# A transformer layer on one core: the residual computed later, look-ups with written-out indices, and half chunks spread over the gate stage

## The chip, the cores and the metric

The kernel runs on one core of one Trainium2 chip. The metric is the device time of one execution in microseconds (us); the median of three executions of the kernel before is 2918.57 us (2915.17 to 2919.74). The engines of the core are PE (matrix products), DVE (vector), ACT (scalar functions and copies), POOL (general, here above all an issuer of DMAs) and SP (issues DMAs). Each runs its own instructions in order.

## The reference

One layer over 1024 tokens (and 16 meta tokens in front) of width 1024, all in float32:

```
h = layer_norm(concat(meta, x))                       # "embedding" norm with gain g and bias b
q, k, v, xr, gr = split(h @ w_in)                     # 3 x 512 and 2 x 512 columns
attn  = stick_breaking_attention(q, k, v)             # 8 heads of 64
lru   = rg_lru(conv4(xr)) * gelu(gr)                  # gated linear recurrence
h = layer_norm(ALPHA * h + concat(rms(attn), rms(lru)) @ w_out)
# PEER: 16384 experts, 8 heads, product keys of 2 x 128
s1, s2 = q1 @ keys1, q2 @ keys2                       # 128 scores each, per head
top 16 of each; top 16 of the sums -> 16 experts (i1 * 128 + i2) and softmax weights g
ffn = sum over heads, experts of g * gelu(down[e] . h) * up[e]
out = layer_norm(ALPHA * h + ffn)
```

## The kernel before

The tokens are 8 blocks of 128. Exact products are made of three reduced ones: every operand x is split into a high part (ACT, L123: wh, dh, v, uh) and a low part (DVE, L124: wl, dl, v, ul), and `mm3` (L126 to L129) issues low·high, high·high, high·low. What PE multiplies in a stage must thus have passed ACT and then DVE. Instructions have an order per engine that is set when the program is built, by a list scheduler that works with estimated durations; on the chip each engine takes its own list strictly in order and waits where an operand is missing.

*Start.* The norm runs in three batches of three blocks (`LNB`): DVE statistics, ACT normalises (L281), PE transposes, ACT applies gain and bias (L292), and hT is stored as high and low part (L295, L297, L298). Beside it `convs` makes the first two projections. Then the residual ALPHA * h is made in token order: `xts[j]` times eg plus eb (L303 to L308; 16 DVE operations on 128x1024), stored to DRAM as `xh_d` by SP, and read again by `lru_load` (L561) when the output projection runs, after the attention.

*Values and recurrence.* `values_w` splits value weights, `values` makes vt in 9 blocks per half, between the pieces of the recurrence (`lru_in`, `lru_gates`). Attention, output projection and second norm follow.

*Query stage* (`queries`). For each of 8 heads and both halves PE makes qt (three pieces, evacuated by ACT, L784) and the scores; DVE takes the top 16 (`topk1`), then of the sums (`topk_pos`), and `topk_look` turns positions into indices: `oh` compares a position with 0 to 15 (L744, against the constant `iotb`), is multiplied by the index repeated 16 times (L745), and is summed by halving (L746 to L749). Between, PE makes chunks of the dense product ahead of time (`run_ahead`, L861; number per step in `RAQ`), and DVE makes dot products with gathered rows (`hyb`).

*Gate stage.* For the 5 dense blocks of tokens the weights are spread over the 16384 experts: 80 groups of 8 tokens, each with two kinds of one-hot tables (DVE: bt, ae; ACT: at, eight copies at L1027), eight matmuls g (L1030), one evacuation (ACT, L1031), one `hyb` step, and one turn of the top-k of the last two blocks (`topk_turn`). After each block `RAG[j]` chunks (6, 7, 6, 6, 6, together 31) are made with `run_ahead`: a chunk is the down product of 128 experts with 640 tokens, two halves of 24 matmuls (dps), a gelu (ACT) and a store of 320 KB to `ge_d`. Four groups fill a gate buffer st, which SP stores to Gd (L1035).

*Dense stage.* 128 chunks: those made ahead (56, `RA`) are loaded from `ge_d`, the others are made here; each is multiplied by its gates (gl, L1142), split, and multiplied by the up rows (ups). Beside it DVE works through the gathered rows of the last blocks (`sparse_units`), given out in proportion to PE's work (`tick`).

## Time and profile before

| | |
|---|---|
| median of 3 executions | 2918.57 us |
| profiled execution, its span | 2921.73 us, 2919.9 us |
| busy: PE, DVE, ACT, POOL | 95%, 85%, 39%, 42% |
| mean granted clock of PE | 0.979 |
| start and norm, then values and recurrence | to about 54 us, to about 240 us |
| attention, output projection | to about 555 us, to about 625 us |
| query stage | 624 to 1047 us |
| gate stage, to the first up matmul | 1047.5 to 1504 us |
| dense stage and last norm | 1504 to 2919.9 us |

The profile names instructions by line of the kernel and by tile (out<-in). Busy shares are of the whole span; a view cut to a window tells what limits a stage. "Idle before" is the time for which an engine had nothing running before an instruction, with the releaser that ended it. A granted clock of 1.0 is 2.4 GHz, 0.5 is 1.2 GHz.

### The profile page before, as it was taken

How to read it: one execution, taken by the hardware profiler on the slowest of the kernel's cores; microseconds unless marked ns; L12 is line 12 of the kernel's file. 1: busy time of each engine (PE TensorE's matmuls, PEld its weight loads, DVE VectorE, ACT ScalarE, POOL GpSimd, SP SyncE). 2: the span in 40 equal slices, each digit the busy share in tenths (PEclk: the TensorE clock that was granted, in tenths of full speed). 3: DMA queues.
4: the chain of work that ended last, by engine and by line, in shares of the span. 5: the costliest groups of instructions: out<-in, count | busy, mean ns of one | idle time of the engine just before them, and what ended most of it. 6: DMA issues, size and time to landing. Idle time of an engine off the chain costs nothing.

```text
span 2919.9 us, 44345 instructions
## 1 busy us (share of the span) xinstructions
PE 2771.6 (95%) x16311; PEld 2490.4 (85%) x16311; DVE 2468.0 (85%) x4768; ACT 1146.0 (39%) x2245; POOL 1224.4 (42%) x1028
## 2 busy tenths in 40 slices
PE   5999999999899987999999999999999999999997
PEld 5998777789899986989988888888888888888886
DVE  8345666769999999689869999999999999999996
ACT  5444554552122268578832222222222232222232
POOL 0002320232333444134325565665555566666653
PEclk9999999999999999899999999999999999999999
DMA  5113134414677778698889999999999999999981
GB/s 176 46 59 88 42 88 151 145 57 148 224 240 230 246 235 276 202 290 252 262 292 351 349 347 353 345 351 361 343 350 355 350 337 358 360 342 369 334 312 73
DMA packets 353946, 736.32 MB, mean 252 GB/s; under 512 B 26032, under 2 KB 164272, under 8 KB 353728
## 3 DMA queue, kind: packets, MB, share of 16 engines
q0 software_dynamic: 113152, 411.16, 39.7%
q1 hardware_dynamic: 235968, 320.23, 32.6%
q8 instruction: 128, 2.10, 0.3%
q10 hardware_dynamic: 4608, 2.10, 0.3%
q14 instruction: 90, 0.74, 0.1%
HBM read 645.24 MB, written 79.69 MB: 248 GB/s over the span
## 4 chain that ended last, share of the span: by engine, by line
PE 50%; DVE 15%; issue 6%; POOL 3%; ACT 3%; DMA 2%; SPq 0%; POOLq 0%; DVEq 0%; ACTq 0%
PE dps L127 6%; PE dps L129 6%; PE dps L128 6%; PE ups L127 6%; PE ups L128 6%; PE ups L129 6%; PE g L1030 5%; DVE row L113 4%; POOL row L898 3%; DVE dl L124 2%; PE keep L129 2%; PE keep L128 2%; PE keep L127 2%; ACT gst L1031 1%; DMA row<-down,idx 1%
## 5 line engine op out<-in xcount | busy, mean ns | idle before, releaser
L127 PE MATMUL dps<-hTd,dl 128*128 128x320 f32 x2048 | 645.2, 315 | 33.8 <-DVE dl L124 26.1
L129 PE MATMUL dps<-hTd,dh 128*128 128x320 f32 x2048 | 641.2, 313 | 0.0
L128 PE MATMUL dps<-hTd,dh 128*128 128x320 f32 x2048 | 641.0, 313 | 0.0
L898 POOL DMA_INDIRECT row<-down,idx x256 | 357.7, 1397 | 226.1 <-DVE act L113 182.0
L898 POOL DMA_INDIRECT row<-up,idx x256 | 343.7, 1342 | 229.2 <-DVE h1s L1086 192.0
L127 PEld LDWEIGHTS dps<-hTd,dl 128*128 128x128 f32 x2048 | 388.9, 190 | 38.4 <-DVE dl L124 20.2
L127 PE MATMUL ups<-uh,wl 128*128 128x512 f32 x1024 | 406.3, 397 | 0.4 <-DVE wl L124 0.4
L128 PE MATMUL ups<-uh,wh 128*128 128x512 f32 x1024 | 406.3, 397 | 0.0
L129 PE MATMUL ups<-ul,wh 128*128 128x512 f32 x1024 | 405.5, 396 | 0.0
L128 PEld LDWEIGHTS dps<-hTd,dh 128*128 128x128 f32 x2048 | 388.9, 190 | 3.0
L129 PEld LDWEIGHTS dps<-hTd,dh 128*128 128x128 f32 x2048 | 388.3, 190 | 0.1
L1086 DVE SCALAR_TENSOR_TENSOR h1s<-row,gws,h1s 128x1024 f32<-128x1024 f32 x256 | 328.3, 1282 | 16.1 <-DMA row<-up,idx 14.0
L113 DVE CUSTOM_DVE_ANT_0 row<-row,h1s 128x1024 f32<-128x1024 f32 x256 | 307.5, 1222 | 33.9 <-DMA row<-down,idx 33.1
L123 ACT ACTIVATE wh<-gl 128x640 fp32r<-128x640 f32 x128 | 101.3, 792 | 575.9 <-DVE gl L1142 315.0
L898 POOL DMA_INDIRECT row<-up,idh x128 | 189.7, 1482 | 305.5 <-DVE acc L1076 95.8
L898 POOL DMA_INDIRECT row<-down,idh x128 | 162.2, 1268 | 245.1 <-DVE ach L113 106.3
L124 DVE TENSOR_TENSOR dl<-raw,dh 128x1024 fp32r<-128x1024 f32 x144 | 179.7, 1248 | 80.5 <-ACT dh L123 80.0
L129 PEld LDWEIGHTS ups<-ul,wh 128*128 128x128 f32 x1024 | 192.8, 188 | 47.3
L127 PEld LDWEIGHTS ups<-uh,wl 128*128 128x128 f32 x1024 | 192.8, 188 | 45.2 <-DVE wl L124 0.8
L128 PEld LDWEIGHTS ups<-uh,wh 128*128 128x128 f32 x1024 | 192.8, 188 | 43.9
L123 ACT ACTIVATE uh<-raw 128x1024 fp32r<-128x1024 f32 x128 | 133.5, 1057 | 191.1 <-PE keep L128 171.2
L1176 DVE TENSOR_TENSOR acc<-acc,ups 128x512 f32<-128x512 f32 x252 | 171.9, 682 | 16.8 <-PE ups L129 16.6
(577 smaller groups left out, 5948.1 us busy)
## 6 DMA issues: line engine op xcount, KB each, us to landing
raw<-downT SPq DMA_DIRECT2D x128, 512.0 KB
raw<-up SPq DMA_DIRECT2D x128, 512.0 KB
Gd<-gst SPq DMA_DIRECT2D x20, 2048.0 KB
gl<-Gd SPq DMA_DIRECT2D x128, 320.0 KB
ge_d<-ge SPq DMA_DIRECT2D x56, 320.0 KB
gex<-ge_d SPq DMA_DIRECT2D x56, 320.0 KB
wraw<-w_in SPq DMA_DIRECT2D x20, 512.0 KB
raw<-wq SPq DMA_DIRECT2D x16, 512.0 KB
```

The costliest lines, as they stand in the source:

```text
L113: return lambda *a, **k: pin(getattr(V, name)(*a, **k))
L123: A.activation(hi, src, AF.Copy)
L124: V.tensor_tensor(lo, src, hi.bitcast(F32), op=ALU.subtract)
L127: PE.matmul(o, ll, rh, start=start, stop=False, **kw)
L128: PE.matmul(o, lh, rh, start=False, stop=False, **kw)
L129: PE.matmul(o, lh, rl, start=False, stop=stop, **kw)
L898: G.indirect_dma_start(out=row, out_offset=None, in_=src, in_offset=bass.IndirectOffsetOnAxis(ap=ix, axis=0))
L1030: PE.matmul(gpt[:, q], bt[:, q], at[:, q], start=True, stop=True)
L1031: A.activation(st[:, :, t8 - t0:t8 - t0 + 8].rearrange("p a t b -> p t a b"), gpt.rearrange("p t (a b) -> p t a b", b=2), AF.Copy)
L1086: pin(V.scalar_tensor_tensor(h1s[:, j], row, gws[:, j, s:s + 1], h1s[:, j], op0=ALU.mult, op1=ALU.add))
L1176: V.tensor_tensor(h1[j][:, hsl], h1[j][:, hsl], ps, op=ALU.add)
```

## The change

Four things. First, SP now stores the normalised block itself (without gain and bias) to `xh_d`, and a generator `residuals` reads it back in half width on POOL's queue, applies gain and bias on DVE, and stores the result to a new `xr_d`; a step of it is taken after each block of `values`. Its tile `rt` has one buffer. Second, in the query stage ACT writes the index sixteenfold (`ibx`), so that the multiplication has a second operand that is read densely; `iotb` holds one table instead of six, and `oh` has one buffer instead of two. Third, 34 instead of 31 chunks are made ahead in the gate stage, by halves: 68 half chunks are given out evenly over the 80 groups (`ahead_turn`). Fourth, the dense stage thus has 3 chunks less to make (RA is 59). Lines below the first hunk move: L744 and L745 become L766 and L767, L1030 becomes L1072.

```diff
@@
 RAQ = {i: 1 + (i > 7) for i in range(1, 16)}
-RAG = (6, 7, 6, 6, 6)
+RAG = 34
 RAM = {7: 2}
-RA = sum(RAM.values()) + sum(RAQ.values()) + sum(RAG)
+RA = sum(RAM.values()) + sum(RAQ.values()) + RAG
 RAS = sorted([1 + 4 * i for i in range(min(RA, 32))] + [2 + 4 * i for i in range(RA - 32)])
@@
     xh_d = dram.tile([S, D], F32, name="xh_d")
+    xr_d = dram.tile([S, D], F32, name="xr_d")
     al_d = dram.tile([KC, P, S], F32, name="al_d")
@@
                     A.activation(xts[j][:n], xts[j][:n], AF.Identity, bias=nm9[:n, j:j + 1], scale=rs9[:n, j:j + 1])
+                    if j > 0:
+                        SY.dma_start(xh_d[(j - 1) * P:j * P, :], xts[j])
                 c0 = 0 if j0 == 0 else NM + (j0 - 1) * P
@@
                     next(gen)
-            eg = load_vec(ga, 0, "eg")
-            eb = load_vec(ga, 1, "eb")
-            A.activation(eg, eg, AF.Copy, scale=ALPHA)
-            A.activation(eb, eb, AF.Copy, scale=ALPHA)
-            for j in range(1, NT + 1):
-                V.tensor_tensor(xts[j], xts[j], eg, op=ALU.mult)
-                V.tensor_tensor(xts[j], xts[j], eb, op=ALU.add)
-                SY.dma_start(xh_d[(j - 1) * P:j * P, :], xts[j])
-
         with ExitStack() as c2:
@@
                 mps = c3.enter_context(tc.tile_pool(name="mps", bufs=1, space=PSUM, reuse_waits="tile"))
+                rx = c3.enter_context(tc.tile_pool(name="rx", bufs=1, reuse_waits="tile"))
                 sp8 = lr.tile([P, 4], F32, name="sp8")
@@

+                def residuals():
+                    for hf in range(2):
+                        cs = slice(hf * 512, hf * 512 + 512)
+                        gb = []
+                        for i in range(2):
+                            t = rx.tile([P, 512], F32, name=f"rv{i}")
+                            G.dma_start(t, vecs[i, cs].partition_broadcast(P))
+                            A.activation(t, t, AF.Copy, scale=ALPHA)
+                            gb.append(t)
+                        for j in range(NT):
+                            t = rx.tile([P, 512], F32, name="rt")
+                            G.dma_start(t, xh_d[j * P:(j + 1) * P, cs])
+                            V.tensor_tensor(t, t, gb[0], op=ALU.mult)
+                            V.tensor_tensor(t, t, gb[1], op=ALU.add)
+                            G.dma_start(xr_d[j * P:(j + 1) * P, cs], t)
+                            yield
+
+                res = residuals()
+
                 def lru_in(i):
@@
                         A.activation(vt[:m, b, half * 256:half * 256 + 256], ps[:m, :256], AF.Copy)
+                        next(res, None)

@@
                     V.tensor_tensor_scan(ts_[i], rs_[i], ys[i], 0.0, op0=ALU.mult, op1=ALU.add)
+                for _ in res:
+                    pass
                 ms = mps.tile([P, NT], F32, name="ms")
@@
                 hr = wr.tile([P, D], F32, name="raw")
-                SY.dma_start(hr, xh_d[j * P:(j + 1) * P, :])
+                SY.dma_start(hr, xr_d[j * P:(j + 1) * P, :])
                 return mh, ml, hr
@@
         tkw = c1.enter_context(tc.tile_pool(name=f"tkw{n}", bufs=wb, side=side, reuse_waits="tile"))
-        iotb = tk.tile([P, n, TOPK, TOPK], BF16, name=f"iotb{n}")
-        G.iota(iotb, pattern=[[0, n], [1, TOPK], [0, TOPK]], base=0, channel_multiplier=0, allow_small_or_imprecise_dtypes=True)
+        iotb = tk.tile([P, TOPK, TOPK], BF16, name=f"iotb{n}")
+        G.iota(iotb, pattern=[[1, TOPK], [0, TOPK]], base=0, channel_multiplier=0, allow_small_or_imprecise_dtypes=True)
         return tk, tkw, iotb
@@
         W.tensor_copy(ib, ii)
+        ibx = []
+        for half in range(2 if n > ST else 0):
+            t = tkw.tile([P, n, TOPK, TOPK], BF16, name="ibx")
+            A.activation(t, ib[:, half].unsqueeze(3).broadcast_to([P, n, TOPK, TOPK]), AF.Copy)
+            ibx.append(t)
         for half in range(2):
             oh = tkw.tile([P, n, TOPK, TOPK], BF16, name="oh", bufs=ohb)
-            W.tensor_tensor(oh, ab[:, half].unsqueeze(2).broadcast_to([P, n, TOPK, TOPK]), iotb[:, :n], op=ALU.is_equal)
-            G.tensor_tensor(oh, oh, ib[:, half].unsqueeze(3).broadcast_to([P, n, TOPK, TOPK]), op=ALU.mult)
+            W.tensor_tensor(oh, ab[:, half].unsqueeze(2).broadcast_to([P, n, TOPK, TOPK]), iotb.unsqueeze(1).broadcast_to([P, n, TOPK, TOPK]), op=ALU.is_equal)
+            G.tensor_tensor(oh, oh, ibx[half] if ibx else ib[:, half].unsqueeze(3).broadcast_to([P, n, TOPK, TOPK]), op=ALU.mult)
             G.tensor_tensor(oh[:, :, 0:8], oh[:, :, 0:8], oh[:, :, 8:16], op=ALU.add)
@@
             hs = slice(h * TOPK, (h + 1) * TOPK)
-            topk_look(V, tkw, iotb, DT, ab, ii, [sel[:, half, :, hs] for half in range(2)], V, 2)
+            topk_look(V, tkw, iotb, DT, ab, ii, [sel[:, half, :, hs] for half in range(2)], V, 1)
             yield
@@
     def down_gelu(c, dps, ge, tick=None):
+        for _ in down_halves(c, dps, ge, tick):
+            pass
+
+    def down_halves(c, dps, ge, tick=None):
         hi, lo = ddn.pop(c)
@@
                 tick(KC * 3 * HN)
+            yield

...

+    def aheads(n):
+        for _ in range(n):
+            c = next(ra)
+            ddn[RAS[c]] = take()
+            ge = geps[0].tile([P, NF], F32, name="ge")
+            for i, _ in enumerate(down_halves(RAS[c], dps1, ge)):
+                if i == 1:
+                    SY.dma_start(ge_d[c], ge)
+                yield
+
     def run_ahead():
-        c = next(ra)
-        ddn[RAS[c]] = take()
-        ge = geps[0].tile([P, NF], F32, name="ge")
-        down_gelu(RAS[c], dps1, ge)
-        SY.dma_start(ge_d[c], ge)
+        for _ in aheads(1):
+            pass

@@
                 turn[1] += 1
+
+        ahead = aheads(RAG)
+        gone = [0]
+
+        def ahead_turn(groups):
+            while gone[0] * groups < turn[0] * 2 * RAG:
+                next(ahead, None)
+                gone[0] += 1

@@
                     topk_turn(DF * P // 8)
+                    ahead_turn(DF * P // 8)
                 blk = (j * P + t0) // GB
                 SY.dma_start(Gd[:, :, blk].rearrange("g p f -> p g f"), st.rearrange("p (g a) t b -> p g (a t b)", a=GI // 2))
-            for c in range(RAG[j]):
-                run_ahead()
+        next(ahead, None)
         hdepth[0] = 0
```

Below, a row is engine order, line, operation, out<-in, shape; "x2" stands for two alike. First DVE at the end of the norm, before: xt are the residual's blocks, y the convolution, v the low part of the value weights, which PE needs next.

```order
L298 TENSOR_TENSOR hT_88<-tm,hT_87 128x384
L306 TENSOR_TENSOR xt<-xt,eg 128x1024 x2
L307 TENSOR_TENSOR xt<-xt,eb 128x1024 x2
L306 TENSOR_TENSOR xt<-xt,eg 128x1024 x2
L307 TENSOR_TENSOR xt<-xt,eb 128x1024 x2
L352 TENSOR_SCALAR y_631<-xr,ch 128x1040
L333 MEMSET t_630 128x4
L352 TENSOR_SCALAR y_632<-xr,ch 128x1040
L354 SCALAR_TENSOR_TENSOR y_631<-xr,ch,y_631 128x1040
L329 TENSOR_SCALAR t_628<-t_627 128x4
L124 TENSOR_TENSOR v_678<-wraw,v_677 128x8x128
```

And after (rt is the residual in half width):

```order
L354 TENSOR_TENSOR rt<-rt,rv_724 128x512
L301 TENSOR_TENSOR hT_89<-tm,hT_88 128x384 x3
L298 CAST hT_88<-tm 128x384
L355 TENSOR_TENSOR rt<-rt,rv_727 128x512
L301 TENSOR_TENSOR hT_89<-tm,hT_88 128x384
L328 MEMSET t_612 128x4
L125 TENSOR_TENSOR v_660<-wraw,v_659 128x8x128
L366 TENSOR_SCALAR y_613<-xr,ch 128x1040
L324 TENSOR_SCALAR t_610<-t_609 128x4
L368 SCALAR_TENSOR_TENSOR y_613<-xr,ch,y_613 128x1040
L325 RECIPROCAL t_610<-t_610 128x4
L125 TENSOR_TENSOR v_660<-wraw,v_659 128x8x128
```

The residual operations no longer stand between the last hT and v; two of the sixteen steps are seen among the hT rows, each with a load in front on POOL's queue.

Second, PE in the gate stage, where the first block's groups go on; before:

```order
L127 MATMUL dps<-hTd_5239,dl 128x320
L128 MATMUL dps<-hTd_5239,dh 128x320
L129 MATMUL dps<-hTd_5240,dh 128x320
L106 MATMUL tr<-ident,sf 128x128 x2
L106 MATMUL tr<-ident,gwd 128x128
L1030 MATMUL g<-at__11171,bt 128x128 x8
L685 MATMUL sc<-sk,qx 128x128 x2
L1030 MATMUL g<-at__11199,bt 128x128 x8
L1030 MATMUL g<-at__11239,bt 128x128 x8
L685 MATMUL sc<-sk,qx 128x128 x2
L1030 MATMUL g<-at__11643,bt 128x128 x8
```

and after:

```order
L129 MATMUL dps<-hTd_5314,dh 128x320
L130 MATMUL dps<-hTd_5315,dh 128x320
L128 MATMUL dps<-hTd_5314,dl 128x320
L129 MATMUL dps<-hTd_5314,dh 128x320
L1072 MATMUL g<-at__11810,bt 128x128
L130 MATMUL dps<-hTd_5315,dh 128x320
L1072 MATMUL g<-at__11810,bt 128x128 x2
L128 MATMUL dps<-hTd_5314,dl 128x320
L1072 MATMUL g<-at__11810,bt 128x128 x3
L129 MATMUL dps<-hTd_5314,dh 128x320
L1072 MATMUL g<-at__11810,bt 128x128 x2
L130 MATMUL dps<-hTd_5315,dh 128x320
```

Before, the down matmuls end here, and groups follow each other until the block is done; after, 24 down matmuls stand between (and partly within) one group's eight g and the next's.

Third, ACT in the query stage of head 7, which also holds the look-up of head 6; before:

```order
L861 ACTIVATE ge<-dps 128x320 x2
L123 ACTIVATE dh<-raw 128x1024
L861 ACTIVATE ge<-dps 128x320 x2
L123 ACTIVATE dh<-raw 128x1024
L784 ACTIVATE qt<-z 128x320 x2
L784 ACTIVATE qt<-z 128x384
L123 ACTIVATE dh<-raw 128x1024
L687 ACTIVATE sb<-sc 128x512
L687 ACTIVATE sb<-sc 128x256
```

and after:

```order
L887 ACTIVATE ge<-dps 128x320 x2
L124 ACTIVATE dh<-raw 128x1024
L887 ACTIVATE ge<-dps 128x320 x2
L124 ACTIVATE dh<-raw 128x1024
L806 ACTIVATE qt<-z 128x320 x2
L762 ACTIVATE ibx<-ib 128x1536 x2
L806 ACTIVATE qt<-z 128x384
L704 ACTIVATE sb<-sc 128x512
L124 ACTIVATE dh<-raw 128x1024
L704 ACTIVATE sb<-sc 128x256
```

Both writes of ibx stand between the second and the third piece of qt.

## Rows read from the trace of the kernel before

**Rows 1.** The page, part 1: busy time and share of the span by engine, instructions.
```profile
PE 2771.6 (95%) x16311; PEld 2490.4 (85%) x16311; DVE 2468.0 (85%) x4768; ACT 1146.0 (39%) x2245; POOL 1224.4 (42%) x1028
```

**Rows 2.** Windows: length; busy by engine (instructions); TensorE's clock, DMA share, GB/s.
```profile
60.00:80.00 20.00, 10.74 (x48) 8.56 (x48) 17.70 (x25) 6.61 (x10) 0.55 (x4) 0.61 0.44 148
80.00:240.00 160.00, 158.30 (x1084) 153.75 (x1083) 59.20 (x77) 70.59 (x100) 4.62 (x11) 1.00 0.19 54
640.00:1044.00 404.00, 373.30 (x2473) 371.28 (x2472) 388.71 (x1565) 95.61 (x169) 136.04 (x125) 0.97 0.64 207
1047.50:1504.00 456.50, 410.62 (x2798) 396.22 (x2796) 376.19 (x974) 341.69 (x840) 152.79 (x109) 0.96 0.82 262
1184.00:1232.00 48.00, 48.00 (x323) 48.00 (x323) 22.05 (x57) 19.29 (x45) 5.50 (x6) 0.96 0.60 203
1316.00:1374.00 58.00, 55.10 (x403) 52.52 (x402) 52.76 (x136) 52.28 (x131) 24.79 (x15) 0.99 0.79 244
1504.00:2840.00 1336.00, 1331.63 (x6897) 1164.01 (x6896) 1255.71 (x1546) 350.15 (x461) 796.79 (x583) 1.00 0.95 348
```

**Rows 3.** Waits of PE, 40 to 80 us: us in total, times, longest.
```profile
PE pp L129 <- DVE v L124: 9.3, 1, 9.3
PE pp L127 <- ACT v L123: 4.3, 1, 4.3
```

**Rows 4.** Timeline of DVE at the start: start us, duration, instruction.
```profile
53.39 0.55 DVE L298 TENSOR_TENSOR hT<-tm,hT 128x384 fp32r<-128x384 f32 x1
...
60.67 2.35 DVE L307 TENSOR_TENSOR xt<-xt,eb 128x1024 f32<-128x1024 f32 x2
...
68.14 1.19 DVE L124 TENSOR_TENSOR v<-wraw,v 128x1024 fp32r<-128x1024 f32 x1
```

**Rows 5.** Timeline of POOL, loads from DRAM and their first reader.
```profile
239.34 0.51 POOL L543 DMA_DIRECT2D QS<-qh  x1 [9.15 <-ACT qh L538]
...
242.90 0.52 POOL L471 CAST qz<-QS 64x128 fp32r<-64x128 f32 x2 [1.44 <-DMA QS<-qh]
```

**Rows 6.** Groups of DVE, 640 to 1044 us: busy us, mean ns, idle before.
```profile
L745 DVE TENSOR_TENSOR oh<-oh,ib 128x1536 bf16<-128x1536 bf16 x16 | 28.0, 1752 | 0.0
...
L744 DVE TENSOR_TENSOR oh<-ab,iotb 128x1536 bf16<-128x1536 bf16 x16 | 15.2, 951 | 0.0
```

**Rows 7.** Groups of ACT, same stretch.
```profile
L123 ACT ACTIVATE dh<-raw 128x1024 fp32r<-128x1024 f32 x40 | 42.0, 1050 | 0.0
...
L687 ACT ACTIVATE sb<-sc 128x512 f32<-128x512 f32 x15 | 8.9, 590 | 2.4 <-remote 2.4
```

**Rows 8.** Timeline of DVE, head 6 of the queries.
```profile
976.20 0.25 DVE L741 CAST ib<-ii 128x192 bf16<-128x192 uint32 x1
```

**Rows 9.** Timeline of ACT, the same place.
```profile
974.22 0.49 ACT L784 ACTIVATE qt<-z 128x384 f32<-128x384 f32 x1 [3.72 <-PE z L127]
```

**Rows 10.** Windows of L1031 alone (one instruction a group of 8 tokens).
```profile
1046.00:1115.00 69.00, 16.10 (x15) 1.00 0.91 287
1115.00:1184.00 69.00, 17.23 (x17) 0.88 0.84 260
1316.00:1374.00 58.00, 15.31 (x14) 0.99 0.79 244
```

**Rows 11.** Windows of L128 alone (one of three matmuls of a down product).
```profile
1046.00:1115.00 69.00, 21.89 (x67) 1.00 0.91 287
1316.00:1374.00 58.00, 17.91 (x54) 0.99 0.79 244
```

**Rows 12.** Timeline of SP's queue at the end of the gate stage.
```profile
1464.91 0.37 SPq L1035 DMA_DIRECT2D Gd<-gst  x1
...
1474.43 1.62 SPq L1117 DMA_DIRECT2D gl<-Gd  x3
```

**Rows 13.** Waits of DVE, 1504 to 2840 us.
```profile
DVE row L113 <- DMA row<-down,idx: 33.1, 43, 2.4
...
DVE h1s L1086 <- DMA row<-up,idx: 14.0, 27, 1.3
```

## Prediction

> **What bounds the kernel now.** I read the page first [rows 1]: one core, PE busy 95% of 2919.9 us, DVE 85%. An average over four very different stages says little, so the next view is the table of windows [rows 2], with one line a stage. From 80 to 240 us (values and recurrence) PE works 158.3 of 160 us. From 640 to 1044 us (the query stage) DVE works 388.7 of 404 us and PE 373.3, so DVE sets the pace and PE has 31 us of holes. From 1047.5 to 1504 us (the gate stage) PE is called busy for 410.6 of 456.5 us, DVE for 376.2, ACT for 341.7: none is full, and the work alternates between stretches limited by different engines. From 1504 us on (the dense stage) PE works 1331.6 of 1336 us. So a gain needs shorter PE work in the dense stage, shorter DVE work in the query stage, better packing in the gate stage, and no hole for PE at the start.
>
> **Part 1, the residual.** The hole at the start is in the waits of PE between 40 and 80 us [rows 3]: 9.3 us for DVE's low half of the value weights and 4.3 us for ACT's high half, 13.6 us together. DVE's rows say why [rows 4]: the residual products, 16 full-width operations at 1.22 us each (a pair takes 2.35), end at 63.0 us; the second split of the value weights, which PE waits for, ends only at 69.3. The last split of hT is over at 53.9 us, and 9.1 us of residual work stands directly behind it. PE then starts cold: the granted clock is 0.61 between 60 and 80 us [rows 2], a mix of the levels of 1.2 and 2.4 GHz, behind those waits.
> In the new order the first value split stands right behind the last split of hT; the second follows two short rows and two of the convolution. By that order PE resumes near 57 us instead of 69.3: 12 us less, plus 2 us or so of cold clock. Against it: 32 half-width operations, at no less than half of 1.22 us each (I take 0.65), and 36 transfers on POOL's queue. There is one rt buffer, so each of the 16 steps is load, two operations, store, next load. [Rows 5] price a load from DRAM on that queue: the first QS is issued at 239.34 us and POOL's copy that needs it begins at 242.90, so 3.5 us. A step is 3.5 + 1.3 + 3.5, about 8 us; sixteen are 133 us, and start near 20 us. The result is first read by the output projection, which comes after the attention, so the end of the chain is covered. Its beginning isn't: steps 1 to 4 stand on DVE between the splits of hT, where steps 3 and 4 are only some 4 us apart. Each can hold the splits by about 4 us. In return 8 full operations (9.8 us) leave that stretch and 8 half ones (5.2) enter it. I take −14 + 2 × 4 − 4, that is −10, and −12 with the wait of step 4 lying beside PE's last convolution pieces. Ends: −17 (no wait) and +8 (all four steps wait 5 us, 20 us against 12).
>
> **Part 2, the look-ups.** The 16 multiplications by a repeated index take 1.752 us each, the 16 comparisons of the same size and type 0.951 [rows 6]. With a dense second operand I expect the comparison's time: 16 × 0.80 = 12.8 us less DVE work in a DVE-bound stage. ACT gets 16 writes of 128x1536. Its rows in this stage are 0.590 us for 512 columns and 1.050 for 1024 [rows 7], so by the same slope 1.5 us, 24 us in all, beside 95.6 busy of 404 [rows 2]. This is cheap as work, but not as order: ACT is served in order, and the writes wait for DVE's cast of the indices, with evacuations of query pieces (qt) behind them. Read against before: for head 6 the cast runs at 976.20 us while the qt that now stands behind the writes ran at 974.22 [rows 8, 9]; qt would be done about 976.5 + 3 + 0.5 = 980 instead of 974.7. PE's scores and then its next chunk stand behind that. Head 5 is alike in the order; in the other heads the cast comes first, or PE waits for the low half of a weight (dl) anyway. So about two stalls of 3 to 5 us on PE, part of which falls into the 31 us of holes that PE has there. I take −7; ends −13 and +6.
>
> **Part 3, the half chunks.** A stretch of nearly pure down work is PE at its pace: 1184 to 1232 us, 323 matmuls in 48.00 us, 0.1486 us each [rows 2]; a chunk has 48, a half 24. A pure gate stretch is the other extreme: 1115 to 1184 us holds 17 groups and no down matmul, 4.06 us a group [rows 10], set by DVE and ACT. The mixed stretch 1316 to 1374 us holds 14 groups and 54 × 3 = 162 down matmuls: 4.14 us a group with 11.6 of them [rows 10, 11]. So 1.72 us of down work a group came almost for nothing. The rest of the down work lies in bursts like that from 1184 us, in which DVE works 22.1 of 48 us. After, the order has 24 at a time, 68 halves for 80 groups, 20.4 a group. If the 8.8 beyond 11.6 cost PE in full, a group takes 4.14 + 1.31 = 5.45 us; if they are hidden, DVE sets the end: 376.2 us + 3 more splits = 380. PE is already called busy 95% there [rows 2], but its gate matmuls then wait between one another for ACT's tables, so some is hidden. I take 5.0: 80 × 5.0 = 400, plus about 22 for what lies before the first group, the last 100 rows (15 us) and what follows. That last piece is a new wait: before, the last store of gate blocks is issued at 1464.91 us and the first load from it at 1474.43 [rows 12], and the 240 matmuls between the last gate matmul and the first up matmul, 36 us, covered that. Now 100 stand there, 15 us, against 9.5 for the store and, as I guess, as much for load and splits: about 4 us uncovered, counted in the 22. So 422 instead of 456.5: −34. Ends: −66 (DVE alone, 390) and +2 (5.45 a group).
> DMA would stand it: 262 GB/s × 456.5 us are 120 MB, and these with 3 MB more in 422 us make 291 GB/s, under the 348 of the dense stage [rows 2].
>
> **Part 4, the dense stage** has 3 chunks less: 3 × 48 × 0.1486 = 21.4 us, nearly all on the path, since PE works all but 4 us there. But DVE's dot products already wait 33.1 us for gathered rows, its sums 14.0 [rows 13], at a DMA share of 0.95 [rows 2], and as many rows must come in less time. I take −17; ends −21 and 0.
>
> Sum: −12 − 7 − 34 − 17 = −70. The profiled execution is 2921.7 us (span 2919.9 + 1.8), so 2851.7; the median of before is 3.1 lower, hence 2849.
>
> **Rivals.**
> (a) *The groups go one after another.* A group needs DVE, then ACT, then PE, then ACT, and PE runs in order: a half chunk in front of a gate block delays ACT's evacuation, and with two buffers everybody waits in turn. Price: 4.06 + 20.4 × 0.1486 = 7.1 us a group at worst, 80 × 7.1 + 22 = 590, the stage 134 slower and the kernel 98, near 3016. It decides from where the stage eats the other 36 us: (456.5 + 36 − 22)/80 = 5.9 us a group. For it: the stretch 1046 to 1115 us, 15 groups with 67 × 3 / 15 = 13.4 down matmuls each, took 4.6 us a group [rows 10, 11]. Against it: 4.14 with 11.6. At 6.2, a little past that point, the stage takes 518 and the time is 2943.
> (b) *The residual loads hold DVE and ACT at the start*: the +8 end of part 1. The first two ACT rows now are the scalings that wait for POOL's loads, ahead of the first normalisation; against it, the first QS of [rows 5] was there within 3.5 us, with four transfers queued. Time 2849 + 20 = 2869.
> The Trainium skill, SBUF — State Buffer (SBUF: two separate sides, the "DVE blocks DMA" trap), speaks for (b): a DMA issued from POOL's queue can't write its descriptors while DVE runs certain copies or casts, and there 620 ns became about 3100. By its figures a step with two such DMAs would be an estimated 5 us longer and the kernel come out near (b). No run here shows it so far: no row of before has a POOL transfer beside the casts of hT.
> (c) *Gathered rows bind the dense stage*, and the three chunks give nothing: 2866. For it the 33.1 us; against it that PE waits for none of it.
> (d) *The look-ups do not do what they say*: ACT's writes wait for the cast, and PE for ACT, so the query stage loses 6: 2862.
>
> **Chances.** Forecast 0.60, its own range 2828 to 2872. (a) 0.15, of it 0.09 beyond 5.9 us; (b) 0.12; (c) 0.08; (d) 0.05. Two of (b) to (d) together reach 2886, all three 2899. Range 2812 to 2900: down to a gate stage at all but its lower end (390), up to these three. A difference under 0.2% (6 us) can't be told from none: faster 0.86, same 0.05, slower 0.09.
>
> **What would show it.** Start: the first value matmul before 60 us, no wait for v over 3 us; wrong if DVE waits for rt between the splits. Query stage: L767 near 0.95 us; fewer than 25 us of holes in PE; wrong if DVE's multiplication waits for ibx or PE for qt. Gate stage: a group every 5.0 us, no burst before the last 100 matmuls, first ups 34 us earlier relative to the stage's start. Dense: about 17 us shorter, row waits not much above 33 us. The forecast fails if a group takes over 5.5 us or PE waits for ACT's tables at most groups.

## The result, and the profile after

The changed kernel takes 2869.66 us (median; 2865.36 to 2876.53), the kernel before 2916.87 us on the same chip: a ratio of 0.9842, 95% interval 0.9817 to 0.9866, so 1.6% faster, about 46 us of the 70 forecast. A second measurement, against other runs of the kernel before, gave 2872.96 us and again 0.9842 (0.9823 to 0.9861). The profiled execution took 2876.5 us, its span is 2874.0.

The page's busy times first; they answer to [rows 1]:

```profile
PE 2748.7 (96%) x16311; PEld 2467.2 (86%) x16311; DVE 2458.4 (86%) x4784; ACT 1160.1 (40%) x2263; POOL 1236.0 (43%) x1064
```

PE has as many matmuls as before. Four events mark where the stages begin, and are the same in every kernel here: POOL's first load of QS (start of the attention), ACT's first qt (query stage), ACT's first gst (gate stage), PE's first ups (dense stage). The tile views, of after (count: shortest/median/longest ns, first and last start in us):

```profile
L560 POOL DMA_DIRECT2D QS<-qh x8: 514/516/519, 242.8 to 423.0; - x8
L806 ACT ACTIVATE qt<-z x48: 419/440/490, 634.7 to 1002.1; 128x320 f32<-128x320 f32 x32, 128x384 f32<-128x384 f32 x16
L1073 ACT ACTIVATE gst<-g x80: 1033/1108/1132, 1055.4 to 1438.2; 128x1024 f32<-128x1024 f32 x80
L128 PE MATMUL ups<-uh,wl x1024: 391/397/628, 1456.1 to 2850.1; 128*128 128x512 f32 x171
```

and the same of before (its QS begins at 239.34, [rows 5]):

```profile
L784 ACT ACTIVATE qt<-z x48: 421/442/490, 631.8 to 1002.4; 128x320 f32<-128x320 f32 x32, 128x384 f32<-128x384 f32 x16
L1031 ACT ACTIVATE gst<-g x80: 1024/1088/1133, 1056.3 to 1463.8; 128x1024 f32<-128x1024 f32 x80
L127 PE MATMUL ups<-uh,wl x1024: 391/397/507, 1504.1 to 2898.2; 128*128 128x512 f32 x171
```

Differences between neighbouring starts give the stages, and with the spans (2919.9, 2874.0) the end:

| stage | before | after | difference | forecast |
|---|---|---|---|---|
| start, to QS | 239.3 | 242.8 | +3.5 | -12 |
| attention, output projection | 392.5 | 391.9 | -0.6 | 0 |
| query stage | 424.5 | 420.7 | -3.8 | -7 |
| gate stage | 447.8 | 400.7 | -47.1 | -34 |
| dense stage, norm | 1415.8 | 1417.9 | +2.1 | -17 |
| sum | 2919.9 | 2874.0 | -45.9 | -70 |

The gate stage holds the whole gain; the other four rows add up to +1.2 us. The windows of after, in the columns of [rows 2]; the stretches of query, gate and dense stage answer to its third, fourth and seventh row:

```profile
60.00:80.00 20.00, 16.94 (x110) 14.71 (x109) 18.25 (x35) 11.04 (x18) 2.77 (x8) 1.00 0.48 146
640.00:1044.00 404.00, 380.84 (x2513) 379.10 (x2512) 382.02 (x1569) 119.64 (x189) 128.38 (x125) 0.97 0.64 210
1055.00:1456.00 401.00, 393.35 (x2912) 384.86 (x2911) 369.96 (x963) 340.23 (x835) 147.22 (x106) 1.00 0.91 289
1456.00:2800.00 1344.00, 1332.86 (x6827) 1156.60 (x6826) 1256.66 (x1550) 341.76 (x457) 800.57 (x583) 1.00 0.95 349
```

In the gate stage PE, which had 46 us of holes [rows 2], is now busy 393 of 401 us. The 79 steps from the first to the last gst take 382.8 us, 4.85 us a group, and the way from the last gst to the first ups shrank from 40.3 to 17.9 us. In the dense stage the table shows 70 fewer matmuls in a window 8 us longer, and the same 349 GB/s at a share of 0.95 (348 before): PE is called busy all the same; the starts of its matmuls, in the part on the dense stage, tell more.

At the start, waits of DVE and of PE between 20 and 250 us (us in total, times, longest) in after; PE's answer to [rows 3]:

```profile
DVE rt L354 <- DMA rt<-xh_d: 58.1, 13, 7.4
```

```profile
PE pp L128 <- ACT gg L437: 6.2, 2, 5.1
PE pp L130 <- DVE hT L301: 5.3, 1, 5.3
...
PE pp L128 <- ACT v L124: 1.5, 1, 1.5
PE pp L130 <- DVE v L125: 0.5, 1, 0.5
```

and PE's wait for gg before, in the same stretch:

```profile
PE pp L127 <- ACT gg L420: 1.6, 1, 1.6
```

PE's 13.6 us for v are down to 2.0, but it waits 5.3 for an hT and 6.2 (1.6 before) for the gates gg of the recurrence, and DVE waits 58 us for rt. DVE's timeline shows where (start, duration, instruction, idle before), and answers to [rows 4]:

```profile
40.26 0.69 DVE L354 TENSOR_TENSOR rt<-rt,rv 128x512 f32<-128x512 f32 x1 [7.06 <-DMA rt<-xh_d]
...
48.84 0.69 DVE L354 TENSOR_TENSOR rt<-rt,rv 128x512 f32<-128x512 f32 x1 [2.11 <-DMA rt<-xh_d]
...
60.02 0.55 DVE L301 TENSOR_TENSOR hT<-tm,hT 128x384 fp32r<-128x384 f32 x1
60.51 1.22 DVE L125 TENSOR_TENSOR v<-wraw,v 128x1024 fp32r<-128x1024 f32 x1
...
163.46 0.69 DVE L354 TENSOR_TENSOR rt<-rt,rv 128x512 f32<-128x512 f32 x1 [7.42 <-DMA rt<-xh_d]
...
164.79 1.23 DVE L420 TENSOR_TENSOR ig<-r 128x1040 f32<-128x1040 f32 x1
...
167.22 1.24 DVE L383 TENSOR_TENSOR y<-y,ig 128x1040 f32<-128x1040 f32 x1
```

The last hT split ends at 60.6 instead of 53.9 us [rows 4], so the first v split comes 7 us after the place the forecast had for it. PE's first four value matmuls need only ACT's half of the weights, and run from 65.06 us (58.90 before). The fifth needs DVE's half; it is the one that waits 9.3 us in [rows 3]. Before and after:

```profile
69.39 0.58 PE L129 MATMUL pp<-v,hT 128*128 128x256 f32 x1 [9.26 <-DVE v L124]
```

```profile
66.33 0.38 PE L130 MATMUL pp<-v,hT 128*128 128x256 f32 x1 [0.52 <-DVE v L125]
```

It comes 3.1 us earlier. The last step of the residual, at 163.46, waits 7.4 us for its load in front of the last part of the recurrence, which DVE runs in order.

A smaller delay lies ahead of all these rows. DVE's first statistics of a whole block of tokens, before and after:

```profile
6.55 1.29 DVE L113 BATCH_NORM_STATS2 lnst<-xt 128x6 f32<-128x512 f32 x2 [1.19 <-DMA xt<-x]
```

```profile
8.36 1.29 DVE L114 BATCH_NORM_STATS2 lnst<-xt 128x6 f32<-128x512 f32 x2 [2.98 <-DMA xt<-x]
```

The block arrives 1.8 us later, and ACT's first normalisation starts at 14.50 us instead of 12.17. It starts between 13.48 and 14.53 in all ten runs here that have the new residual chain, and between 11.97 and 12.30 in the four that don't. What is new beside that load are POOL's two loads of rv, issued at 1.62 us; no run left out only these.

The look-ups in the query stage, groups of DVE and ACT after (busy us, mean ns, idle before), answer to [rows 6]:

```profile
L767 DVE TENSOR_TENSOR oh<-oh,ibx 128x1536 bf16<-128x1536 bf16 x16 | 15.2, 953 | 0.3
...
L762 ACT ACTIVATE ibx<-ib 128x1536 bf16<-128x1536 bf16 x16 | 23.2, 1477 | 40.3 <-DVE ib L758 40.3
```

PE's waits there, 640 to 1044 us, after:

```profile
PE dps L128 <- DVE dl L125: 12.7, 5, 6.4
PE sc L702 <- ACT qt L806: 10.5, 3, 5.9
```

and before:

```profile
PE dps L127 <- DVE dl L124: 26.1, 5, 13.3
PE z L127 <- DVE dl L124: 4.2, 3, 1.4
```

### The profile page after: what moved, and what is told of

It is laid out like the page before. It is cut to its first block, busy times and chain, and to the rows that moved or that the text cites. A ratio compares the mean times of both kernels' runs of the same rounds, so it can differ in the third digit from the quotient of the medians.

```text
span 2874.0 us, 44494 instructions
## 1 busy us (share of the span) xinstructions
PE 2748.7 (96%) x16311; PEld 2467.2 (86%) x16311; DVE 2458.4 (86%) x4784; ACT 1160.1 (40%) x2263; POOL 1236.0 (43%) x1064
## 4 chain that ended last, share of the span: by engine, by line
PE 27%; DVE 17%; issue 15%; POOL 9%; DMA 9%; ACT 2%; POOLq 0%; DVEq 0%; ACTq 0%; SPq 0%
POOL row L932 9%; PE g L1072 5%; DVE row L114 4%; PE dps L128 4%; PE dps L130 4%; PE dps L129 4%; DMA row<-up,idx 3%; DMA row<-up,idh 3%; DMA row<-down,idx 2%; PE ups L128 2%; PE ups L130 2%; PE ups L129 2%; DVE dl L125 2%; DVE h1s L1128 1%; PE z L128 1%
## 5 line engine op out<-in xcount | busy, mean ns | idle before, releaser
L128 PE MATMUL dps<-hTd,dl 128*128 128x320 f32 x2048 | 648.4, 317 | 25.3 <-DVE dl L125 12.7
L128 PE MATMUL ups<-uh,wl 128*128 128x512 f32 x1024 | 409.4, 400 | 7.9 <-DVE acc L1218 5.1
L128 PEld LDWEIGHTS dps<-hTd,dl 128*128 128x128 f32 x2048 | 389.0, 190 | 31.0 <-ACT gex L887 14.0
L932 POOL DMA_INDIRECT row<-down,idh x128 | 153.4, 1199 | 250.5 <-DVE ach L114 87.5
L128 PEld LDWEIGHTS ups<-uh,wl 128*128 128x128 f32 x1024 | 193.6, 189 | 57.5 <-DVE acc L1218 9.7
L1218 DVE TENSOR_TENSOR acc<-acc,ups 128x512 f32<-128x512 f32 x252 | 171.4, 680 | 10.2 <-PE ups L130 10.1
L124 ACT ACTIVATE dh<-raw 128x1024 fp32r<-128x1024 f32 x144 | 151.7, 1053 | 52.6 <-DMA raw<-downT 52.5
```

The lines of the kernel that those rows point to most:

```text
L124: A.activation(hi, src, AF.Copy)
L128: PE.matmul(o, ll, rh, start=start, stop=False, **kw)
L932: G.indirect_dma_start(out=row, out_offset=None, in_=src, in_offset=bass.IndirectOffsetOnAxis(ap=ix, axis=0))
L1218: V.tensor_tensor(h1[j][:, hsl], h1[j][:, hsl], ps, op=ALU.add)
```

## The experiments

Each kernel ran four or five times beside the kernel before; ratios are to it. The stages are taken by the four marks above:

| kernel | ratio (95%) | start | query | gate | dense |
|---|---|---|---|---|---|
| after | 0.9842 (0.9817-0.9866) | 242.8 | 420.7 | 400.7 | 1417.9 |
| after, again | 0.9842 (0.9823-0.9861) | 239.3 | 422.2 | 401.6 | 1414.1 |
| spread34: chunks alone | 0.9799 (0.9778-0.9821) | 237.0 | 421.9 | 394.4 | 1413.4 |
| no_ibx: chunks, residual | 0.9800 (0.9776-0.9824) | 246.9 | 425.6 | 394.1 | 1414.4 |
| no_residual: chunks, look-ups | 0.9809 (0.9789-0.9829) | 238.9 | 423.3 | 400.5 | 1415.7 |
| rag31 | 0.9829 (0.9813-0.9844) | 241.0 | 426.4 | 385.9 | 1425.7 |
| rtpool | 0.9870 (0.9852-0.9887) | 250.1 | 423.1 | 401.1 | 1413.4 |
| ulskip | 0.9869 (0.9848-0.9890) | 243.9 | 419.7 | 400.8 | 1423.9 |
| geonce | 0.9820 (0.9799-0.9840) | 240.6 | 419.7 | 400.2 | 1405.7 |
| ibxearly | 0.9829 (0.9810-0.9848) | 240.9 | 420.2 | 400.3 | 1411.2 |
| poolhalf | 0.9829 (0.9812-0.9847) | 244.8 | 422.2 | 394.5 | 1412.7 |
| resbypool | 0.9782 (0.9758-0.9806) | 233.0 | 422.2 | 394.6 | 1408.7 |
| resbypool_ibx | 0.9813 (0.9789-0.9837) | 234.8 | 423.0 | 400.5 | 1408.2 |

The two profiles of the same kernel (after) differ by 3.5 us at the start and 3.8 in the dense stage: a difference of that size in one profile proves nothing. In the ten runs of the table whose dense stage is the same (all but rag31, ulskip and geonce) that stage takes 1408.2 to 1417.9 us. The gate stage repeats within 1 us.

**The parts, one undone at a time.** no_residual: the changed kernel with the residual of before.

```diff
-                    if j > 0:
-                        SY.dma_start(xh_d[(j - 1) * P:j * P, :], xts[j])
...
+            for j in range(1, NT + 1):
+                V.tensor_tensor(xts[j], xts[j], eg, op=ALU.mult)
+                V.tensor_tensor(xts[j], xts[j], eb, op=ALU.add)
+                SY.dma_start(xh_d[(j - 1) * P:j * P, :], xts[j])
...
-                        next(res, None)
```

> The changed kernel with the residual made as before (16 full-width DVE operations behind the norm, SP stores), all else as changed. My theory: the residual steps cost more than they saved, because DVE waits 58 us for rt loads, four times between the splits of hT and once in front of the recurrence's tail, so that the attention begins 3.5 us later than before. By it this kernel takes 2866 us (2862 to 2869), first QS load near 239 us instead of 242.8. Rival: the residual's own work gained about 12 us as forecast and something later gave it back; then this kernel is 10 us or more slower than the changed one, 2880.

Measured: 2864.57 us, with the first QS at 238.9, as the theory had it. The new residual gives nothing; if anything it costs some us.

no_ibx: the changed kernel without ACT's writes; DVE multiplies by the repeated index, and oh has two buffers as before.

```diff
-        for half in range(2 if n > ST else 0):
+        for half in range(0):
...
-            topk_look(V, tkw, iotb, DT, ab, ii, [sel[:, half, :, hs] for half in range(2)], V, 1)
+            topk_look(V, tkw, iotb, DT, ab, ii, [sel[:, half, :, hs] for half in range(2)], V, 2)
```

> The changed kernel without the indices written out (ACT writes nothing, the multiplication reads the repeated index, oh has two buffers again). Theory: the look-ups' net gain is about 4 us (12.8 us of DVE work saved, two thirds of it lost again because PE waits 10.5 us for qt pieces behind ACT's writes): 2874 us, and PE's waits for scores behind qt go to zero while those for dl go back to 26 us. Rival: the shift of 3.8 us that the query stage shows comes from elsewhere (order, clock), and the total stays at 2870 or falls.

Measured: 2864.63 us, so the theory (2874) failed. PE's waits for scores are gone and those for dl are back at 24.2 us, as expected, and the query stage is 4.9 us longer than in after (3.4 than in its repetition); but the gate stage is 6.6 shorter.

spread34: both edits above, so the kernel before with the half chunks alone (iotb keeps its one table).

> The kernel before with one part of the change alone: 34 chunks made ahead, spread as halves over the groups; residual and look-ups as before. Theory: this part holds the whole net gain, since taking away the residual part made the changed kernel some 9 us faster and taking away the look-up part cost nothing: 2856 to 2864 us, gate stage to first up matmul 395 us from the first group. Rival: the look-up part did bring its 4 to 5 us in the query stage, and the equality of its removal is noise of the residual chain: then this is 2866 to 2872.

Measured: 2861.09 us; 0.9799 × 2920.66 is 59 us below its kernel before. The half chunks alone bring more than the whole change. Each of the other two parts beside them costs 0 to 3 us, less than can be told apart; both together cost about 12 (0.9842 against 0.9799, and the interval of the second measurement of after lies beyond that of spread34). No run shows why the two together should cost more than their sum.

rag31: as many chunks ahead as before, but spread.

```diff
-RAG = 34
+RAG = 31
```

> The changed kernel with 31 instead of 34 chunks made ahead in the gate stage, still spread as halves. Theory A: the dense stage is no longer limited by PE but by what its DMAs bring (gathered rows, weights, about 350 GB/s), so three chunks more there cost nothing, while the gate stage, now PE-bound (busy 398.8 of 409 us), gets 15 to 21 us shorter: 2852 us, dense stage 1418 us as in the changed kernel. Rival B: the dense stage is still PE-bound and its 2 us more are accidental: then it grows by 17 to 21 us and the total stays within 5 us of 2870.

Measured: 2871.66 us, level with after. The gate stage is 14.8 us shorter, query and dense stages 5.7 and 7.8 longer (4.2 and 11.6 against the repetition). B's total held, its dense stage did not; three chunks made ahead move time from one stage to another and give none. The spreading is what pays.

**The start.** rtpool: the two operations of a step on POOL instead of DVE, since 58 us of DVE's waits are for loads that POOL's queue brings (two memsets go from POOL to DVE, so that POOL isn't later for them).

```diff
-                            V.tensor_tensor(t, t, gb[0], op=ALU.mult)
-                            V.tensor_tensor(t, t, gb[1], op=ALU.add)
+                            G.tensor_tensor(t, t, gb[0], op=ALU.mult)
+                            G.tensor_tensor(t, t, gb[1], op=ALU.add)
```

> The changed kernel with the two operations of each residual step on POOL instead of DVE (and two small memsets moved from POOL to DVE so that they do not stand behind it). Same transfers, same single buffer. Theory: the loss at the start is DVE waiting in order for rt loads; without that the first value matmul comes near 57 to 60 us, the first QS load near 227 to 230 us, and the total is 2855 to 2858. Rival: the transfers themselves (POOL queue beside the norm's loads) or the late first normalisation (2.3 us) cause it; then the first QS stays at 239 us or later and the total above 2866.

Measured: 2882.3 us, slower than after; my expectation was 25 us off. The waits of ACT and PE, 20 to 250 us, show why:

```profile
ACT rv L349 <- DMA rv<-vecs: 20.1, 2, 18.9
```

```profile
PE pp L128 <- ACT vt L400: 15.5, 1, 15.5
```

The scaling of rv had stayed on ACT: the second half's rv is loaded by POOL only after the first eight steps, and ACT, in order, holds PE's vt evacuations behind it. Here one instruction that waits for a DMA on an engine that evacuates cost more than the 58 us that DVE spent waiting.

resbypool: that scaling on POOL too, and no ibx.

```diff
-                            A.activation(t, t, AF.Copy, scale=ALPHA)
+                            G.tensor_scalar(t, t, ALPHA, None, op0=ALU.mult)
```

> The changed kernel without the written-out indices, and with the whole residual chain on POOL (the transfers as changed; both operations and the scaling of gain and bias on POOL; two small memsets on DVE instead). Neither DVE nor ACT now waits for an rt or rv load. Theory: the start lost its gain only because DVE (58 us of waits) and, in the run with POOL's operations alone, ACT (18.9 us behind the second pair of vectors) stand in order behind those loads; by it the first QS load comes at 228 to 234 us and the total is 2852 to 2857. Rival: the loads themselves slow the norm and the values (late first normalisation, DMA competition); then the first QS load stays at 238 us or later and the total at 2860 or more.

Measured: 2853.47 us, ratio 0.9782, the lowest here (its interval overlaps those of spread34 and no_ibx), and the start at 233.0 us. POOL takes most of the same waits (POOL, 20 to 250 us):

```profile
POOL rt L354 <- DMA rt<-xh_d: 45.4, 16, 5.2
```

but nobody stands behind them. DVE is through with hT before 55 us (timeline of DVE, resbypool):

```profile
53.83 1.03 DVE L301 TENSOR_TENSOR hT<-tm,hT 128x384 fp32r<-128x384 f32 x2
54.89 2.18 DVE L125 TENSOR_TENSOR v<-wraw,v 128x1024 fp32r<-128x1024 f32 x1
...
60.12 1.19 DVE L125 TENSOR_TENSOR v<-wraw,v 128x1024 fp32r<-128x1024 f32 x1
```

This is the place that the forecast had for the first v split. PE's fifth value matmul runs at 61.37 us, 8.0 earlier than before, and the first QS 6 earlier. How far PE is at any time can be counted, since every kernel issues 1344 matmuls before the first QS. In resbypool the 300th starts 10.0 us and the 800th 10.1 us earlier than before, the 1000th only 6.4. So the start gives most of the 12 us; what is lost is lost at the recurrence's end, where PE waits 3.8 us for gg (1.6 before) and DVE's products stand beside POOL's last residual steps. In after the same matmuls start 4.5 and 2.9 us earlier and 3.4 later, in its repetition 6.5 and 4.9 earlier and level.

poolhalf: spread34, with three of the eight residual blocks multiplied in place by POOL, without DRAM in between.

```diff
+                R = V if j < 6 else G
-                V.tensor_tensor(xts[j], xts[j], eg, op=ALU.mult)
-                V.tensor_tensor(xts[j], xts[j], eb, op=ALU.add)
+                R.tensor_tensor(xts[j], xts[j], eg, op=ALU.mult)
+                R.tensor_tensor(xts[j], xts[j], eb, op=ALU.add)
```

> The kernel before with the spread half chunks alone, and three of the eight blocks of the residual made by POOL in place (no loads, no extra stores). Theory: the hole at the start comes from the 9 us of residual work behind the last split of hT; with six of sixteen operations on POOL (2.45 us each, done by about 54 us) the value weights are split about 6 to 8 us earlier: first QS load near 231 us, total 2853 to 2857. Rival: DVE and POOL slow each other, or the stores are late; then 2860 to 2866.

Measured: 2868.65 us, a miss of some 13 us, and above the rival's range too. Timeline of POOL in poolhalf:

```profile
45.71 14.06 POOL L307 TENSOR_TENSOR xt<-xt,eg 128x1024 f32<-128x1024 f32 x2 [43.76 <-DVE xt L307]
...
64.31 2.34 POOL L307 TENSOR_TENSOR xt<-xt,eg 128x1024 f32<-128x1024 f32 x1
```

and of DVE:

```profile
66.69 2.94 DVE L353 TENSOR_SCALAR y<-xr,ch 128x1040 f32<-128x1040 f32 x1 [9.14 <-POOL xt L307]
```

Two of POOL's operations took 14.06 us (10.76 and 3.34) while DVE ran its own two-input products, one alone 2.34; DVE then waited 9.1 us for POOL, and PE 15.9 for v.

**The look-ups.** ibxearly: the cast and ACT's writes one step of the top-k earlier, before the sums are sorted.

```diff
             cand = topk_cand(tkw, DT, vv)
+            pre = topk_ib(V, tkw, DT, ii)
             yield
```

> The changed kernel with the cast and the two ACT writes of indices a step earlier in the program (beside the sums of scores, before the second top 16), so that ACT waits less for the cast in front of the query pieces. Theory: the look-ups' gain was lost to PE's wait for scores behind the third piece (10.5 us); here that wait falls under 3 us and the total is 2861 to 2866. Rival: query and gate stage together are limited by PE's work as soon as DVE is relieved, so a wait less in the one comes back in the other: 2868 to 2873.

Measured: 2867.1 us, between the two ranges; query and gate stage as in after (420.2, 400.3). PE's wait for qt, 640 to 1044 us, only halved:

```profile
PE sc L702 <- ACT qt L811: 5.9, 3, 3.5
```

and other waits took its place: PE's waits there are 22.4 us in all, 23.2 in after. Moving the writes one step earlier gains nothing; that their place costs nothing isn't shown.

resbypool_ibx: resbypool with the writes of ibx as in after.

> The best kernel so far (whole residual chain on POOL, spread half chunks, 2853.5 us) with the written-out indices added back as in the change. Theory: they relieve DVE by 12.8 us in the query stage, but PE gets it back as waits for query pieces and as a gate stage 6 us longer; net nothing or worse, 2853 to 2861 us, gate stage to the first up matmul near 400 us instead of 394.6. Rival: the equality in the earlier runs came from the residual chain's scatter, and the look-ups gain the 4 to 5 us of the query stage: 2846 to 2850.

Measured: 2865.98 us, 0.9813 against 0.9782 (the intervals overlap). With and without: query 423.0 and 422.2, gate 400.5 and 394.6. Three pairs now differ by the look-ups (after and no_ibx, no_residual and spread34, these two), and in each the gate stage is about 6 us longer with them. The query stage is shorter with them in the first pair only; in the other two it is 1.4 and 0.8 us longer. Each pair differs in oh's buffers too (one or two), and no run separates these from the writes. What is seen of it: the scheduler, which has ACT's writes in its plan, leaves fewer down matmuls in the query stage. Windows of tile dps alone on PE, query and gate stage, after:

```profile
636.00:1055.00 419.00, 199.31 (x1264) 0.97 0.63 208
1055.00:1456.00 401.00, 283.92 (x1573) 1.00 0.91 289
```

and spread34:

```profile
636.00:1050.00 414.00, 197.89 (x1280) 0.97 0.64 212
1050.00:1443.00 393.00, 274.38 (x1552) 1.00 0.92 293
```

21 more stand in the gate stage, where PE has no room. At 0.1486 us each [rows 2] they weigh 3 us, half of the 6. (PE is called busy with dps 9.5 us longer, but a matmul's busy time covers its neighbours'.) No run put only these matmuls back, so even that half is likely and not shown, and the other half is open.

**The dense stage.** DVE theory: its sums and dot products bind. DMA theory: what the queues bring binds. ulskip: every fourth pair of up blocks has no low part (PE multiplies the high part in its place), 32 subtractions of DVE fewer.

```diff
-            lo = upp.tile([P, 2, 512], F32R, name="ul")
-            split(hi, lo, raw)
+            if m % 4:
+                lo = upp.tile([P, 2, 512], F32R, name="ul")
+                split(hi, lo, raw)
+            else:
+                lo = hi
+                A.activation(hi, raw, AF.Copy)
```

> The changed kernel, but for every fourth pair of up blocks the low part is not made (DVE makes 32 fewer 128x1024 subtractions, 38 us; PE multiplies the high part in its place; same DMAs, same PE work). Theory D: the dense stage is limited by DVE, whose work and row waits fill it (1256.7 us busy of 1344 and over 60 us waiting for rows): the stage falls from 1418 us by 15 to 21, to where PE alone (about 1397) stops it; total 2850 to 2856. Rival T: it is limited by what the DMAs bring; DVE merely waits longer for rows, and the total stays at 2867 to 2873. Rival P: PE; no change either.

Measured: 2881.13 us, slower than after by 8 us in the ratio, and its dense stage not shorter (1423.9). Waits of DVE in the dense stage, ulskip (1456.6 to 2807 us):

```profile
DVE row L114 <- DMA row<-down,idx: 48.3, 59, 2.5
DVE h1s L1128 <- DMA row<-up,idx: 38.0, 41, 3.5
```

and after (1456 to 2800 us), which answer to [rows 13]:

```profile
DVE row L114 <- DMA row<-down,idx: 38.2, 50, 2.2
DVE h1s L1128 <- DMA row<-up,idx: 25.4, 32, 3.2
```

DVE is busy 30 us less in the stage, and waits 23 us longer for gathered rows. Less work for DVE alone thus brought nothing. Since the kernel became slower, and why isn't explained, this run doesn't exclude DVE by itself.

geonce: of the 59 chunks made ahead the first one's result is loaded and used for all, so 58 loads of 320 KB are left out.

```diff
+                if "ge" not in once:
+                    once["ge"] = gex0.tile([P, NF], F32, name="gex")
+                    SY.dma_start(once["ge"], ge_d[RAS.index(c)])
+                ges[c] = once["ge"]
+                return
```

> The changed kernel, but the dense stage loads one of the 59 stored chunks once and uses it for all of them (58 loads of 320 KB, 18.6 MB of about 470, are left out; same PE, DVE and ACT work). Theory T (DMA throughput): 4% fewer bytes at the same 350 GB/s take up to 54 us less, cut to about 17 to 21 by PE: total 2850 to 2856, DVE's row waits nearly gone. Theory D (DVE): its 60 us of row waits shrink in part, the stage loses 5 to 10 us: 2860 to 2866. If rows are bound by the latency of a gather with five buffers, nothing changes: 2867 to 2873.

Measured: 2865.69 us, the dense stage 1405.7, which is 12.2 us less than in after (8.4 less than in its repetition). The window of the dense stage:

```profile
1451.70:2784.00 1332.30, 1327.48 (x6830) 1154.83 (x6830) 1254.01 (x1549) 341.73 (x457) 810.15 (x584) 1.00 0.93 338
```

That is under the 17 to 21 us of theory T, and the total lies in the range of theory D; DVE's row waits, 36.7 and 19.0 us, are far from gone. It is also only 2.5 us less than in resbypool_ibx, whose dense stage is that of after. So fewer bytes may shorten the stage a little; this run doesn't show it clear of the noise.

What PE does in the stage can be read from the starts of its matmuls. Two in a row of 320 columns (dps) start 147 ns apart, two of 512 columns (ups and keep) 234 ns, medians that are the same in all kernels here. By these distances, up to the last up matmul, the work of before (3360 and 3840 matmuls) is 1392 us of 1399, which leaves 6.5 us of holes. In after it is 1370.5 us (3212 and 3840) of 1398.7, and the holes are 28.2 us. So PE did set the pace before, and the three chunks did take 21.7 us of its work; exactly as much came back as holes. The holes are 18 to 28 us in the other runs with this dense stage, 14.8 in rag31 (work 1391.7), 16.0 in geonce and 34.1 in ulskip. Something else is thus level with PE. What came late is seen on ACT, which splits the down weights for PE; its wait for them, before (1504 to 2840 us) and after (1456 to 2800 us):

```profile
ACT dh L123 <- DMA raw<-downT: 5.4, 5, 2.6
```

```profile
ACT dh L124 <- DMA raw<-downT: 52.5, 24, 5.0
```

It is 30.3 us in rag31, 32.1 in geonce and 71.0 in ulskip, so it goes with the holes. This speaks for the transfers, at a share of 0.95 before and after; no run isolates them.

**The repetition.** after_again is the changed kernel.

> The changed kernel again, beside the two others on one chip, to compare them. All theories: 2866 to 2874 us, first QS load between 240 and 247 us, since the seven runs with this residual chain differ by that much there.

Measured: 2872.96 us, as the table says; it sets how much one profile's stages can be trusted.

## Why the prediction came out as it did

The direction, the largest term and the range held; the size and the other three terms did not. That the range held is in part luck: start, query and dense stage fell short by some 38 us together, and the gate stage gave 13 more than its term. 2869.66 us lies just inside the forecast's own upper end (2872), the second measurement just outside.

*Start, -12 forecast, 0 to +3.5 measured.* Two steps failed. The first is the price of the steps at the beginning: "2 × 4" us of waits were allowed for, and the two that lie among the hT splits are 7.06 and 2.11, 9.2 together; but "4" us of work less on DVE did not offset them, and the norm itself begins 2.3 us later, which the sum has at nothing: the last hT split ends 6.7 us late. The fifth value matmul, the one that had waited, gains 3.1 us (69.39 to 66.33) instead of 12. The 12 was also high by the forecast's own order: the second v split stands behind the first and two rows of the convolution, about 4.5 us from the last hT split to its end in after's durations, so PE could resume near 58.5 us and not 57. The second is "the end of the chain is covered". A step does take about 8 us where nothing else holds it (7.4 to 10), sixteen end near 165 us, and the forecast looked at who reads the result, not at what stands behind the last step on DVE: the tail of the recurrence, whose multiplication by ig runs at 167.22 where before it ran at 161.96 (the row of DVE, before):

```profile
161.96 1.24 DVE L369 TENSOR_TENSOR y<-y,ig 128x1040 f32<-128x1040 f32 x1 [23.71 <-ACT ig L367]
```

From there the delay passes to ACT and its gates gg, and PE waits 6.2 us for them. So the gain was given back, and up to 3.5 us more. Rival (b) happened, at 12 to 15 of its 20 us; but the loads of rt held DVE alone. ACT's first two scalings held nothing: the row in front of them already waits for DVE until 12.04 us. resbypool shows the cause: the same transfers, with nothing urgent behind their waits, put PE 10 us ahead and give a start of 233.0.

The Trainium skill's trap cited with (b) would lengthen POOL's transfers beside DVE's casts. It isn't what made the load at 33 to 40 us long: DVE ran nothing from 33.2 to 40.26 us, while the DMA engines were busy to a share of 0.75 (0.01 before), SP's stores to xh_d among their work. In resbypool a load issued at 51.58 us is read at 54.62, 3.0 us, with two casts of hT beside it. No run here shows the trap.

*Query stage, -7 forecast, -3.8 here, and nothing in two of three pairs.* The durations were right (953 and 1477 ns against 0.95 and 1.5 us), and so was the place of the stalls (sc waits 10.5 us for qt in 3 waits; two of 3 to 5 us were forecast). PE's holes are 23 us, under the 25 named. What failed is the size of these stalls and what follows: PE's waits for dl fell by 13.4 us and those for qt came in their place, and outside the stage the gate stage is 6 us longer with the look-ups, which the sum has at nothing. So they cost about as much as they give, or more. Rival (d) is right in its sign, not in its place.

*Gate stage, -34 forecast, -47.1 measured.* The mechanism was right and the size too small: 4.85 us a group for 5.0, and 17.9 us for the tail. In the forecast a part of the 8.8 down matmuls a group beyond 11.6 still cost PE; PE's holes before took nearly all of them, and it ended at 98% busy: of the 13 us beyond the forecast the groups make 12 (80 × 0.15). DMA went to 289 GB/s, 291 forecast. Rival (a) is excluded: the groups do not go one after another. Without the look-ups the stage takes 394.4, a gain of 53.

*Dense stage, -17 forecast, +2.1 measured (-1.7 in the repetition).* This is the outcome of rival (c), and the largest part of the shortfall. Failed is the step "nearly all on the path, since PE works all but 4 us there": PE did set the pace before, with 6.5 us of holes, but the step takes it that PE still sets it with 21 us less work. Another limit lay within those 21 us, and the holes grew to 28.2. The transfers stood at a share of 0.95; a chunk made ahead spares 512 KB of down weights but costs 320 KB of ge_d, so 3 chunks spare 0.6 MB, under 2 us at 349 GB/s. Worked out in bytes the term is near nothing, as measured. That the transfers are this other limit is likely by ACT's waits for weights, and not shown: geonce spared bytes and gained no more than the noise, and ulskip relieved DVE and gained nothing. Rival (c) names the gathered rows; DVE's waits for these grew from 47 to 64 us, ACT's for weights from 15 to 71.

The sum by undoing: the chunks -59, forecast as -51 (gate and dense together); residual and look-ups +12, forecast as -19.

## What to carry to other kernels

Before work is moved beside other work, list what stands behind each of its waiting instructions on its own in-order engine, to the end of the chain; the engine for a chain of load, compute and store is the one with nothing urgent behind it. Where PE and the transfers of a stage are both nearly full, count what an edit spares in bytes as well as in matmuls, and expect no more than the smaller of the two. A full engine sets the pace only until it is relieved: ask how far below the next limit lies. Spreading work into the holes of a stage paid fully; the version with the spread chunks and the whole residual on POOL, without the written-out indices, has the lowest time found: 2853.47 us, 0.9782 (0.9758 to 0.9806), though not clear of the chunks alone (0.9799).

## What the runs showed of the hardware that was not expected

POOL and DVE hold each other up. In poolhalf two products of 128x1024 on POOL took 14.06 us beside DVE's products of two operands and 2.34 us each without; DVE's last product beside them took 3.26 us instead of 1.22. In resbypool a v split of DVE, from 54.89 us on, took 2.18 us beside two POOL products of 128x512, against 1.19 alone:

```profile
54.62 1.37 POOL L354 TENSOR_TENSOR rt<-rt,rv 128x512 f32<-128x512 f32 x1 [2.48 <-DMA rt<-xh_d]
56.07 2.15 POOL L355 TENSOR_TENSOR rt<-rt,rv 128x512 f32<-128x512 f32 x1
```

The shortest such POOL products there take 1.26 us. The Trainium skill, SBUF — State Buffer (Who interferes with whom), says that a DVE instruction with two inputs in SBUF contends with a GpSimd instruction that reads SBUF. These traces agree, and give the price here: three times the duration for the pair on POOL, not quite twice for DVE's split.
